# Feed-forward of a two-layer encoder: eight parts projected down one by one, or together by seven block products

## The chip, the cores and the metric

The kernel runs on one core of a Trainium2 chip. The metric is the device time of one execution in microseconds (us), the median of several runs. Engines are named as in the profile: PE is TensorE's matmul stream and PEld its weight loads, DVE is VectorE, ACT is ScalarE, POOL is GpSimd, SP is SyncE, which here issues all the DMAs on one queue in order. Every engine works through its own instructions in a fixed order and waits where an operand or a buffer is not there yet.

## The reference, cut to what matters

A two-layer encoder, width 1024, is applied to a prompt of 256 tokens and a sample of 512. Each layer modulates its normalised input by a condition (adaptive norm), runs a mixer (layer 0: mLSTM; layer 1: windowed attention), adds it, normalises and modulates again, and runs a feed-forward with a convolution over the tokens:

```
def conv_ffn(h, w_up, conv_w, conv_b, w_down):
    u = h @ w_up
    u = lax.conv_general_dilated(u, conv_w[:, None, :], window_strides=(1,),
                                 padding=((CONV_WIDTH // 2, CONV_WIDTH // 2),),
                                 ...
    g = u[..., :D_FF]
    val = u[..., D_FF:]
    return (jax.nn.silu(g) * val) @ w_down
```

`D_FF` is 2816, the convolution is three tokens wide and works per channel, all values are float32. The result is added to the stream with a gate from the condition.

## The kernel before, in words

**Layout.** Activations lie with channels on the 128 partitions and the 768 tokens of both sequences along the free axis. A float32 product is made from three matmuls in a format of fewer bits: both operands are split into a high part (a cast on ACT, L260) and a low part (a subtraction on DVE, L261), and PE adds high x high, high x low and low x high (L254, or L1169, L1170, L1172 in the up projection).

**Weights** lie in DRAM in units of 128 x 2048, loaded as two halves of 128 x 1024 (512 KB, L269) into a ring of five buffers called `raw`, and split into rings of three `whi` and three `wlo`. Other rings: `slab` (six large buffers), `nt` (eight of 128 x 384 or so), and in PSUM four `pa` buffers in turn and four banks, in the feed-forward at fixed places.

**Feed-forward.** The 2816 channels of each of gate and value are cut into 11 parts (`NPART`) of 256 + 256. `up(p)` makes a part's projection, convolution, gate and product; `down(p)` multiplies the product's 256 channels by the part's unit of down weights and adds the 1024 x 768 result to the stream. The loop at the end of `ffn` runs `down` one part behind `up`: up(0), up(1), down(0), up(2), down(1), ..., up(10), down(9), down(10).

`up` of parts 1 to 10 is made of two `pair`s. A pair takes a 2 x 2 block view of the product (two rows of 128 channels, the inner dimension in two halves of 512, the tokens in two halves of 384) and makes it by seven block products in place of eight (Strassen's scheme in Winograd's form). The seven weight operands come from POOL (four additions and subtractions of 128 x 512, L1202, L1205, L1206, L1214), the seven token operands were made once in the layer's head. A pair is seven `quarters` of 12 matmuls of 384 columns; ACT copies PSUM banks on between them (L1218, L1223, L1229, L1240) and evicts rows (L1182), DVE adds two rows (L1242, L1243). `conv` is one activation on ACT (L1387) and two multiply-adds on DVE (L1389, L1390) per row; `silu` (L1397) is issued inside the next pair; `product` multiplies gate and value on POOL (L1402, 128 x 772) and splits the result on ACT and DVE (L260, L261).

`down(p)` below part 10 loads and splits two weight tiles and runs, for 8 blocks of output channels, 512 sample and 256 prompt tokens, 2 x 3 matmuls; each of the 16 results in PSUM is added to the stream by one DVE instruction (`resid`, L590). `down(10)` goes over three ranges of 256 tokens and starts the next norm.

**What sets the order.** Inside the head of the feed-forward and inside the attention's blocks the PE order is written by hand; elsewhere a list scheduler places each engine's instructions from the program's order and its own estimates, once, when the kernel is built. SP's queue is in order too: a DMA that waits for a buffer or for data holds all later ones.

**The mixers.** The mLSTM has a loop over four heads; in it, while the projections of q and k run, steps of the adaptive norm's weights for later (`adaln_g`, `adaln_v`: loads of 512 KB and multiply-adds on DVE, L506) are issued by `self.step(...)`. POOL does small operations there: masks (L708), powers of the normalisation (L826), products with the output gate (L850). The attention goes over 48 steps of blocks, in which scores, transposes and values of a block are three steps apart (`LAG`), and POOL normalises each block's probabilities (L1000).

## Time and profile before

| | |
|---|---|
| median of 3 runs | 1844.86 us (1842.9 to 1848.7) |
| the profiled execution | 1843.78 us |
| its span, first to last instruction | 1842.0 us |
| busy in the span: PE, DVE, ACT, POOL | 97%, 74%, 49%, 26% |
| mean granted clock of PE | 0.994 |
| DMA | 184.48 MB, mean 100 GB/s |

The stages lie in the span like this (stretches that were cut by eye, with the busy time of the engines in each):

| stretch, us | what | PE | DVE | ACT | POOL |
|---|---|---|---|---|---|
| 0 to 38 | start | 22.7 | 12.5 | 11.9 | 8.9 |
| 38 to 505 | mLSTM and adaptive norms | 459.2 | 328.6 | 205.5 | 47.1 |
| 505 to 548 | output projection, head of feed-forward 0 | 41.9 | 37.3 | 22.2 | 9.3 |
| 548 to 1043 | feed-forward 0 | 489.9 | 390.4 | 241.2 | 180.5 |
| 1043 to 1230 | attention | 184.1 | 130.7 | 122.3 | 53.5 |
| 1230 to 1340 | output projection, head of feed-forward 1 | 107.4 | 81.1 | 56.0 | 12.8 |
| 1340 to 1842 | feed-forward 1 | 488.0 | 386.4 | 236.2 | 176.0 |

How to read the lines of the profile. A window's row gives its length and, for each engine, the busy time and the number of instructions, then the granted clock of PE (1.00 is full), the share of the DMA engines' time and GB/s. A group's row gives the line of the kernel, engine, operation, output <- inputs, the shape, the count, the busy time in us, the mean of one in ns, and behind the last bar the engine's idle time ahead of these instructions with what ended it. A timeline's row gives start, duration, engine, line and operation, and in brackets the idle time ahead of it. A DMA row gives the number, the size and the median us from issue to landing. Matmuls overlap in PE's pipeline, so that the distance of two starts, and not a duration, is what one costs.

### The profile page before, as it was taken

The page shows a single profiled execution, that of the slowest core. Times are in us where ns is not written, and L with a number is a line of the kernel's source. Part 1 is how long each engine was busy: PE and PEld are TensorE (multiplying, and loading weights), DVE is VectorE, ACT ScalarE, POOL GpSimd, SP SyncE. Part 2 cuts the span into 40 slices and gives each one's busy share as a digit, 9 for nine tenths or more (in the row PEclk, how much of TensorE's full clock was granted, in tenths as well). Part 3 has the DMA queues.
Part 4 walks back from the last instruction along what each step waited for, and adds up shares of the span by engine and source line. Part 5 has one row for each costly group of instructions (what it writes and reads, how often), then busy time and mean ns, then how long its engine had stood idle before and what let it go on. Part 6 is the DMA issues. An engine that isn't in the chain of part 4 may idle for free.

```text
span 1842.0 us, 28931 instructions
## 1 busy us (share of the span) xinstructions
PE 1793.2 (97%) x11290; PEld 1657.4 (90%) x11290; DVE 1367.0 (74%) x2101; ACT 895.3 (49%) x1815; POOL 488.0 (26%) x386
## 2 busy tenths in 40 slices
PE   6999999999999999999999999999999999999997
PEld 3987887889998999999999999889989999999997
DVE  4755676886689877777777757766898777777776
ACT  4443443354456444444444556765564444444443
POOL 1001001021024333333331313430144333333322
PEclk9999999999999999999999999999999999999999
DMA  8344566546312221222223321124122222222212
GB/s 330 119 145 134 172 195 221 164 138 219 101 46 74 76 61 66 69 69 69 69 69 93 104 83 50 53 94 129 50 86 69 69 69 69 69 69 70 69 35 69
DMA packets 64245, 184.48 MB, mean 100 GB/s; under 512 B 6167, under 2 KB 23831, under 8 KB 64108
## 3 DMA queue, kind: packets, MB, share of 16 engines
q1 hardware_dynamic: 64108, 182.63, 30.8%
q8 instruction: 89, 1.46, 0.3%
q14 instruction: 48, 0.39, 0.1%
HBM read 176.17 MB, written 6.43 MB: 99 GB/s over the span
## 4 chain that ended last, share of the span: by engine, by line
PE 86%; DVE 6%; DMA 3%; ACT 2%; issue 1%; POOL 1%; SPq 0%; POOLq 0%; ACTq 0%; DVEq 0%
PE ps L254 27%; PE pa L254 25%; PE ps L1169 10%; PE ps L1172 10%; PE ps L1170 10%; PE pa L1008 1%; DMA slab<-in_adaln_w_dram 1%; DMA raw<-in_w_dram 1%; DVE wlo L261 1%; DVE ada L506 1%; DVE slab L590 1%; DMA raw<-in_adaln_w_dram 0%; PE pa L1172 0%; PE pa L1169 0%; PE pa L1170 0%
## 5 line engine op out<-in xcount | busy, mean ns | idle before, releaser
L260 ACT CAST whi<-raw 128x1024 fp32r<-128x1024 f32 x237 | 247.9, 1048 | 350.4 <-PE pa L254 161.4
L261 DVE TENSOR_TENSOR wlo<-raw,whi 128x1024 fp32r<-128x1024 f32 x237 | 316.6, 1337 | 119.8 <-ACT whi L260 117.3
L254 PE MATMUL pa<-slab,whi 128*128 128x256 f32 (+1 forms) x1472 | 346.6, 331 | 3.2 <-DVE slab L590 3.2
L254 PEld LDWEIGHTS pa<-slab,whi 128*128 128x128 f32 x1472 | 252.7, 188 | 27.5 <-DVE slab L590 4.5
L590 DVE SCALAR_TENSOR_TENSOR slab<-pa,mod,slab 128x256 f32<-128x256 f32 (+1 forms) x368 | 211.2, 592 | 70.8 <-PE pa L254 70.5
L254 PE MATMUL pa<-slab,wlo 128*128 128x256 f32 (+1 forms) x736 | 233.9, 330 | 0.0
L254 PE MATMUL ps<-zh,whi 128*128 128x256 f32 (+1 forms) x560 | 189.0, 339 | 2.3 <-ACT whi L260 1.7
L254 PE MATMUL ps<-zh,wlo 128*128 128x256 f32 (+1 forms) x560 | 184.1, 330 | 2.0 <-DVE wlo L261 2.0
L254 PE MATMUL ps<-zl,whi 128*128 128x256 f32 (+1 forms) x560 | 185.1, 332 | 0.0
L1169 PE MATMUL ps<-zh,whi 128*128 128x384 f32 x504 | 172.3, 342 | 3.6 <-ACT nt L1240 1.8
L1170 PE MATMUL ps<-zl,whi 128*128 128x384 f32 x504 | 169.9, 337 | 0.8 <-DVE zl L1126 0.8
L1172 PE MATMUL ps<-zh,wlo 128*128 128x384 f32 x504 | 168.9, 335 | 0.0
L254 PEld LDWEIGHTS pa<-slab,wlo 128*128 128x128 f32 x736 | 138.5, 188 | 13.1 <-DVE wlo L261 0.4
L1205 POOL TENSOR_TENSOR raw<-raw,raw 128x512 f32<-128x512 f32 x40 | 52.2, 1305 | 330.8 <-DVE wlo L261 259.4
L254 PE MATMUL ps<-slab,whi 128*128 128x384 f32 x512 | 132.0, 339 | 0.9 <-DVE slab L261 0.5
L1402 POOL TENSOR_TENSOR slab<-slab 128x772 f32<-128x772 f32 x44 | 86.5, 1967 | 164.6 <-DVE slab L1390 152.7
L1389 DVE SCALAR_TENSOR_TENSOR slab<-slab,cstt,slab 128x771 f32<-128x771 f32 x88 | 103.6, 1179 | 26.6 <-ACT slab L1387 26.5
L254 PEld LDWEIGHTS ps<-zh,whi 128*128 128x128 f32 x560 | 107.4, 192 | 15.9 <-issue 4.4
L506 DVE SCALAR_TENSOR_TENSOR ada<-raw,silc,ada 128x1024 f32<-128x1024 f32 x84 | 110.6, 1354 | 14.9 <-DMA raw<-in_adaln_w_dram 14.8
L1202 POOL TENSOR_TENSOR raw<-raw 128x512 f32<-128x512 f32 x40 | 68.5, 1712 | 200.1 <-DMA raw<-in_w_dram 169.7
L254 PEld LDWEIGHTS ps<-zh,wlo 128*128 128x128 f32 x560 | 107.2, 192 | 12.2 <-DVE wlo L261 2.9
L254 PEld LDWEIGHTS ps<-zl,whi 128*128 128x128 f32 x560 | 107.4, 192 | 11.9 <-issue 3.4
(291 smaller groups left out, 4265.7 us busy)
## 6 DMA issues: line engine op xcount, KB each, us to landing
raw<-in_w_dram SPq DMA_DIRECT2D x208, 512.0 KB, 3.7
raw<-in_adaln_w_dram SPq DMA_DIRECT2D x84, 512.0 KB, 4.6
slab<-in_x_dram SPq DMA_DIRECT2D x12, 512.0 KB, 6.8
slab<-in_adaln_w_dram SPq DMA_DIRECT2D x12, 512.0 KB, 10.3
slab<-mrows SPq DMA_DIRECT2D x8, 384.0 KB, 5.3
xs<-slab SPq DMA_DIRECT2D x6, 512.0 KB, 3.6
bt<-brow SPq DMA_DIRECT2D x16, 192.0 KB, 3.0
slab<-xs SPq DMA_DIRECT2D x6, 512.0 KB, 6.9
```

The costliest lines, as they stand in the source:

```text
L254: self.nc.tensor.matmul(out, lhsT, rhs, start=start, stop=stop)
L260: nc.scalar.copy(hi, src)
L261: return nc.vector.tensor_tensor(lo, src, hi.bitcast(F32), ALU.subtract)
L506: stt(acc[:, s], row, w, acc[:, s], ALU.mult, ALU.add)
L590: self.nc.vector.scalar_tensor_tensor(x, o, self.mod[l][:, gc + c, q : q + 1], x, ALU.mult, ALU.add)
L1169: mm(o, wh[:, k], hi[k], start=start and k == 0, stop=False, skip_group_check=True)
L1170: mm(o, wh[:, k], lo[k], start=False, stop=False, skip_group_check=True)
L1172: mm(o, wl[:, k], hi[k], start=False, stop=k == 3, skip_group_check=True)
L1202: tt(q[2], q[2], q[3], ALU.add)
L1205: tt(q[0], q[2], q[0], ALU.subtract)
L1389: stt(y[:, 1:], u[:, :-1], w(0), y[:, 1:], ALU.mult, ALU.add)
L1402: nc.gpsimd.tensor_tensor(y, y, yrow[:, j], ALU.mult)
```

## The change

Parts 0, 1 and 10 keep their `down`. For parts 2 to 9 (`SOLO` = 2, `NBLK` = 8) it is replaced:

- `sums(l)` makes, on POOL, the four weight operands of Winograd's form for each of the eight units of down weights, in the `raw` ring, and stores them to a DRAM scratch `sd`. It is spread over the mixer: layer 0's in the mLSTM's loop (five steps with each q or k of heads 1 and up), layer 1's in the attention (one step per block from the third).
- `operands(yrow, k)` takes the place of `product` in these parts: POOL multiplies gate and value (four instructions), DVE makes four sums, and the seven token operands of the part (128 x 7 x 384) are stored to a DRAM scratch `yd`.
- `blocked` runs after the last pair: seven block products, each over the eight parts, for four blocks of output channels and 384 tokens, 96 matmuls each. It loads weights (from the weights as they are, or from `sd`) and operands from `yd`, splits them on ACT and DVE, keeps sums in eight PSUM buffers, and adds the results to the stream.
- Then comes `down(10)`. The PE order inside `blocked` is written by hand.

The diff, without the lines of constants that stand in the text above:

```diff
                     if h:
                         self.step(self.fillp)
+                        self.step(self.fills, 5)
                 qk.append(t)
...
         done = 0
+        extra = self.sums(1)
         with self.tc.manual_schedule(engines={mybir.EngineType.PE}):
...
                 if x < nb:
                     scores(blocks[x])
+                if x > 1:
+                    next(extra, None)
                 if LAG <= x < nb + LAG:
                     flip(blocks[x - LAG])
...
+        for _ in extra:
+            pass
         return act
...
+    def sums(self, l):
+
+        nc = self.nc
+        tt = nc.gpsimd.tensor_tensor
+        self.sd[l] = sd = self.dp.tile([NBLK, P, 2048], F32, name=f"sd{l}")
+        for k in range(NBLK):
+            u = U_FFN + (l * NPART + SOLO + k) * 3 + 2
+            r = [self.load(u, h) for h in range(2)]
+            s2, s4, s1, s3 = (t[:, 512 * i : 512 * (i + 1)] for t in r for i in range(2))
+            yield
+            tt(s1, s1, s3, ALU.add)
+            yield
+            tt(s2, s1, s2, ALU.subtract)
+            yield
+            tt(s4, s4, s2, ALU.subtract)
+            nc.sync.dma_start(sd[k, :, :1024], r[0])
+            yield
+            tt(s3, s3, s2, ALU.subtract)
+            nc.sync.dma_start(sd[k, :, 1024:], r[1])
+            yield
+
+    def blocked(self, l, xt, u, yd):
+
+        nc = self.nc
+        w, sd = self.io["w"], self.sd[l]
+
+        def given(i):
+            return lambda k: w[u + 3 * k : u + 3 * k + 4 : 3, :, 512 * i : 512 * (i + 1)]
+
+        def summed(i):
+            return lambda k: sd[k : k + 2, :, 512 * i : 512 * (i + 1)]
+
+        stream = [
+            (given(0), 0), (given(1), 2), (summed(0), 4), (summed(1), 3), (summed(3), 1), (summed(2), 6), (given(3), 5),
+        ]
+        K = range(NBLK)
+        parts = {}
+
+        def ready(i):
+            if i >= len(stream):
+                return
+            src, z = stream[i]
+            ys = self.slab([P, NBLK, H])
+            for k in K[::4]:
+                nc.sync.dma_start(ys[:, k : k + 4], yd[k : k + 4, :, z].rearrange("k p t -> p k t"))
+            for k in K:
+                if k % 2 == 0:
+                    raw = self.stg.tile([P, 2, 512], F32, tag="raw", name=self.nm("raw"), bufs=5)
+                    nc.sync.dma_start(raw, src(k).rearrange("k p c -> p k c"))
+                    wt = self.split(raw.rearrange("p k c -> p (k c)"))
+                y = [self.tmp([P, H], R) for _ in range(2)]
+                self.fp_copy_split(*y, ys[:, k])
+                parts[i, k] = [t[:, 512 * (k % 2) : 512 * (k % 2 + 1)] for t in wt], y
+
+        X = [self.pa()[:, :H] for _ in range(4)]
+        Y = [self.bank[c][:, :H] for c in range(4)]
+
+        def add(c, c0, o):
+            for p0, p1, q in pieces(c0, c0 + H):
+                self.resid(xt, o[:, p0 - c0 : p1 - c0], l, 40, c, (p0, p1, q))
+
+        late = [(c, k) for k in K[:-2] for c in range(4)] + [(c, k) for c in range(4) for k in K[-2:]]
+        soon = [(c, k) for c in range(4) for k in K[:2]] + [(c, k) for k in K[2:] for c in range(4)]
+        steps = [
+            (X, late, True, lambda c: nc.scalar.copy(Y[c], X[c])),
+            (X, soon, False, lambda c: add(c, 0, X[c])),
+            (Y, late, False, lambda c: nc.scalar.copy(X[c], Y[c])),
+            (Y, soon, False, lambda c: add(c, H, Y[c])),
+            (X, late, False, lambda c: add(c + 4, H, X[c])),
+            (Y, late, True, lambda c: (add(c, H, Y[c]), add(c + 4, H, Y[c]))),
+            (X, late, False, lambda c: add(c + 4, 0, X[c])),
+        ]
+        mm = nc.tensor.matmul
+        for i, (o, order, start, done) in enumerate(steps):
+            for j in (0, 1) if i == 0 else (i + 1,):
+                ready(j)
+            with self.tc.manual_schedule(engines={mybir.EngineType.PE}):
+                for c, k in order:
+                    (wh, wl), (yh, yl) = parts[i, k]
+                    cs = slice(c * P, (c + 1) * P)
+                    mm(o[c], wh[:, cs], yh, start=start and k == 0, stop=False, skip_group_check=True)
+                    mm(o[c], wh[:, cs], yl, start=False, stop=False, skip_group_check=True)
+                    mm(o[c], wl[:, cs], yh, start=False, stop=k == K[-1], skip_group_check=True)
+                    if k == K[-1]:
+                        done(c)
...
+        yd = self.dp.tile([NBLK, P, 7, H], F32, name=f"yd{l}")
+
+        def operands(yrow, k):
+
+            s = self.slab([P, 7, H])
+            for j in range(2):
+                row = s[:, 2 * j : 2 * j + 2].rearrange("p z t -> p (z t)")
+                for p0, p1, _ in pieces(0, T):
+                    b = slice(col(p0), col(p0) + p1 - p0)
+                    nc.gpsimd.tensor_tensor(row[:, p0:p1], yrow[:, 2 + j, b], yrow[:, j, b], ALU.mult)
+            b11, t3, b21, b22, t2, t4, t1 = (s[:, z] for z in range(7))
+            tt = nc.vector.tensor_tensor
+            tt(t3, b22, t3, ALU.subtract)
+            tt(t2, b11, t3, ALU.add)
+            tt(t4, b21, t2, ALU.subtract)
+            tt(t1, b22, t2, ALU.subtract)
+            nc.sync.dma_start(yd[k], s)
+
...
-            g = self.slab([P, 2, 2, TG], R)
+            g = None if SOLO <= p < SOLO + NBLK else self.slab([P, 2, 2, TG], R)
...
-            if p:
+            if g is None:
+                operands(yrow, p - SOLO)
+            elif p:
                 product(yrow, g)
...
             if prev is not None:
                 down(*prev)
-            prev = (p, g)
+            prev = (p, g) if g is not None else None
+        self.blocked(l, xt, u0 + 3 * SOLO + 2, yd)
         down(*prev)
...
+        self.fills = self.sums(0)
         act = self.mlstm(pool, gates, xt)
-        for _ in chain(self.fillp, self.fill):
+        for _ in chain(self.fillp, self.fill, self.fills):
             pass
```

More of the change, by code (lines that the diff above doesn't have):

```diff
@@ L35 @@
 NPART = FC // 2
+SOLO = 2
+NBLK = 8
 EPS = 1e-6
@@ L184, in __init__ @@
         self.early, self.begun = {}, {}
+        self.sd = {}
     def start(self, rng, gen):
```

## Prediction

> **What bounds the kernel now.** I read the page's first part, then the windows of the feed-forward's steady stretch, then the single instructions.
>
> ```profile
> span 1842.0 us, 28931 instructions
> ...
> PE 1793.2 (97%) x11290; PEld 1657.4 (90%) x11290; DVE 1367.0 (74%) x2101; ACT 895.3 (49%) x1815; POOL 488.0 (26%) x386
> ```
>
> PE is busy 97% of the span, so time is won only where PE has less to do, and lost wherever PE is made to wait. The windows show three consecutive parts of feed-forward 0, and, for later, the two mixers.
>
> ```profile
> core 0: us, PE busy (x) PEld busy (x) DVE busy (x) ACT busy (x) POOL busy (x), PEclk, DMA share, GB/s
> 623.50:669.90 46.40, 46.20 (x264) 43.88 (x263) 34.34 (x40) 21.30 (x35) 16.40 (x10) 1.00 0.20 65
> 669.90:716.34 46.44, 46.44 (x265) 44.03 (x265) 35.08 (x40) 21.50 (x35) 16.50 (x10) 1.00 0.22 69
> 716.34:762.75 46.41, 46.41 (x265) 43.99 (x265) 35.76 (x42) 21.56 (x35) 17.42 (x10) 1.00 0.23 68
> 124.00:300.00 176.00, 171.74 (x1210) 146.46 (x1210) 116.72 (x214) 71.78 (x196) 11.68 (x9) 0.99 0.54 172
> 300.00:412.00 112.00, 110.21 (x740) 96.69 (x739) 92.23 (x139) 49.43 (x120) 18.61 (x14) 1.00 0.54 177
> 1096.00:1215.00 119.00, 118.41 (x989) 106.99 (x988) 90.15 (x285) 85.93 (x285) 46.27 (x80) 1.00 0.18 52
> ```
>
> A part takes 46.4 us and PE has no gap in it. The same holds, within a few per cent, in the mLSTM (124 to 412) and in the windowed attention (1096 to 1215): whatever the change puts there must stay off PE's path.
>
> **The matmuls.** The change removes `down` for eight parts of each layer and adds seven block products, each of 8 parts x 4 output blocks x 3 = 96 matmuls of 384 columns. The trace has such matmuls in the up projection; from the first row below to the last lie 66 steps, (661.92 − 650.36)/66 = 0.175 us each.
>
> ```profile
> 650.36 0.34 PE L1169 MATMUL ps<-zh,whi 128*128 128x384 f32 x1
> ...
> 661.92 0.34 PE L1170 MATMUL ps<-zl,whi 128*128 128x384 f32 x1
> ```
>
> A part's two pairs are 168 such matmuls: 29.4 us. The `down` beside them is what is left of the period, 46.4 − 29.4 = 17.0 us. Eight of them are 136.0 us; seven products are 7 x 96 x 0.175 = 117.6 us. So 18.4 us per layer are to be had, **36.8 us** for both: an eighth of the down work, less what is lost around it.
>
> **The stretch without down.** While parts 3 to 10 go up, nothing lies between two pairs any more, and everything else has 29.4 us in place of 46.4. One part's groups (669.90 to 716.34):
>
> ```profile
> L261 DVE TENSOR_TENSOR wlo<-raw,whi 128x1024 fp32r<-128x1024 f32 x8 | 11.3, 1415 | 5.5 <-ACT whi L260 5.3
> ...
> L260 ACT CAST whi<-raw 128x1024 fp32r<-128x1024 f32 x9 | 9.4, 1049 | 16.3 <-PE pa L254 8.4 <-PE ps L1170 4.1 <-POOL raw L1206 3.7
> ...
> L590 DVE SCALAR_TENSOR_TENSOR slab<-pa,mod,slab 128x512 f32<-128x512 f32 x8 | 5.9, 744 | 1.8 <-PE pa L254 1.8
> ...
> L1206 POOL TENSOR_TENSOR raw<-raw 128x512 f32<-128x512 f32 x2 | 3.9, 1954 | 0.1
> ...
> L1402 POOL TENSOR_TENSOR slab<-slab 128x772 f32<-128x772 f32 x2 | 3.7, 1856 | 6.4 <-DVE slab L1390 6.4
> ...
> L590 DVE SCALAR_TENSOR_TENSOR slab<-pa,mod,slab 128x256 f32<-128x256 f32 x8 | 3.7, 479 | 2.2 <-PE pa L254 2.2
> ...
> L1205 POOL TENSOR_TENSOR raw<-raw,raw 128x512 f32<-128x512 f32 x2 | 2.6, 1296 | 15.3 <-DVE wlo L261 15.3
> ...
> L261 DVE TENSOR_TENSOR slab<-slab,slab 128x772 fp32r<-128x772 f32 x2 | 2.3, 1174 | 0.0
> ...
> L260 ACT CAST slab<-slab 128x772 fp32r<-128x772 f32 x2 | 1.7, 830 | 0.5 <-POOL slab L1402 0.5
> ...
> L1242 DVE TENSOR_TENSOR slab<-ps,nt 128x384 f32<-128x384 f32 x2 | 1.1, 550 | 0.4 <-PE ps L1172 0.4
> ...
> L1223 ACT COPY nt<-ps 128x384 f32<-128x384 f32 x2 | 0.9, 475 | 0.0
> ```
>
> DVE loses 16 residual adds (9.6 us), two weight splits (2.8) and two operand splits (2.3), and gains four 128x384 subtractions or additions of 0.55: 35.1 − 14.7 + 2.2 = 22.6 of 29.4 us. ACT loses two weight casts and two operand casts: 21.5 − 3.8 = 17.7. POOL swaps two products (3.7) for four, two of 512 and two of 256 columns. The 512s cost 1.30 to 1.95 each by the two POOL rows, the 256s about half; that is 4 to 6, so 17 to 19 of 29.4. No engine becomes the bound. But PE waits for single tiles: the weight split that needs POOL's last sum had the whole `down` as cover and now has, worked out by hand in DVE's new order, some 2 us, and the PSUM copy in the middle of a pair stands on ACT behind a weight cast with almost none. I bound the stall by 0 (both in time) and 1.5 us a part (cast 1.05 plus copy 0.47, both bare), and take **0.2**, near the lower end, since PE shows no gap in the rows above with the same order within a pair: 16 x 0.2 = 3.2 us.
>
> **From the last pair into the block products.** Here PE has nothing of its own to fill with: before, `down(9)` lay there; now product 0 follows the pair directly, in PE's written order. By the new instruction order, product 0's first token cast on ACT stands behind the two operand casts of part 10, these wait for POOL's two products, and the second of those for the convolution of the last row. The load of product 0's token operands is on SP's queue behind two weight loads, the second of which waits for the split of the pair's last weight tile. The same chain stands in the trace of before at the end of layer 0's part 10, where `down(9)` hid it:
>
> ```profile
> 998.32 0.33 PE L1172 MATMUL ps<-zh,wlo 128*128 128x384 f32 x1
> ...
> 999.47 0.54 ACT L1182 COPY slab<-ps 128x128 f32<-128x128 f32 x2
> 1000.04 1.03 ACT L1387 ACTIVATE slab<-slab,cstt 128x772 f32<-128x772 f32 x1
> ...
> 1002.54 1.01 DVE L1389 SCALAR_TENSOR_TENSOR slab<-slab,cstt,slab 128x771 f32<-128x771 f32 x1
> ...
> 1006.06 1.00 DVE L1390 SCALAR_TENSOR_TENSOR slab<-slab,cstt,slab 128x771 f32<-128x771 f32 x1
> ...
> 1007.21 1.86 POOL L1402 TENSOR_TENSOR slab<-slab 128x772 f32<-128x772 f32 x1 [6.33 <-DVE slab L1390]
> ...
> 1009.10 0.84 ACT L260 CAST slab<-slab 128x772 fp32r<-128x772 f32 x1 [1.37 <-POOL slab L1402]
> ```
>
> From the pair's end (998.65) to 1009.94 that is 11.3 us. About 4 of them were DVE's residual adds in between, which are gone. Without them: 1001.07 convolution on ACT, +2.0 on DVE, +1.9 POOL, +0.85 cast, +0.48 token cast, +0.55 its low half on DVE: 6.9 + 1.4 = about 8.3 us from the pair's end to the first matmul. The load, from 2.4 us behind the pair's end (cast 1.05, split 1.25 to 1.4), lands by these rows:
>
> ```profile
> raw<-in_w_dram SPq DMA_DIRECT2D x208, 512.0 KB, 3.7
> ...
> slab<-mrows SPq DMA_DIRECT2D x8, 384.0 KB, 5.3
> xs<-slab SPq DMA_DIRECT2D x6, 512.0 KB, 3.6
> ```
>
> It is 768 KB behind 512 KB, in short runs: between 3.7 and twice 5.3 us, so 6 to 13 us behind the pair's end. Both ends meet around 9 us: **9 us per layer**, bounds 7 and 13. Then the clock:
>
> ```profile
> 40.00:42.00 2.00, 2.00 (x11) 2.00 (x11) 2.00 (x8) 2.00 (x5) 0.00 (x0) 0.50 0.63 252
> ...
> 1058.00:1061.00 3.00, 0.83 (x4) 0.84 (x5) 2.92 (x7) 2.96 (x9) 0.00 (x0) 0.89 0.00 0
> 1061.00:1064.00 3.00, 3.00 (x17) 3.00 (x16) 2.90 (x7) 1.40 (x4) 0.00 (x0) 0.54 0.32 85
> ```
>
> After a gap of 2.2 us the next 3 us ran at 0.54: (1 − 0.54) x 3 = 1.4 us lost. I take **1.5 us** per layer, bounds 0 and 3. In sum 10.5 per layer, **21 us**. The Trainium skill ("TensorE: Matmul & The Clock Gate", section "Why this matters for your kernels") warns of PE gaps over about 3 us, after which the clock is at half until PE has been busy for a window of about 3.4 us; by that page the loss would be some 1.7 us a gap, an estimate, and the sum 0.4 us longer. The row at 1058 shows the drop after a shorter gap than that.
>
> **The products themselves.** Per 16.8 us a product wants 2 MB of weights and 1.5 MB of operands, 3.67 MB with KB of 1024, or 218 GB/s. That is more than the 172 to 177 of the mLSTM windows and less than the 252 of the window at 40. DVE has four weight splits, eight token splits and some adds (5.7 + 4.4 + 2 to 4), ACT 4.2 + 3.8 + 2, of 16.8 us. I take no stall; bounds 0 and, if only 177 GB/s came, 20.7 − 16.8 = 3.9 us for each of 14 products.
>
> **The sums of weights**, eight rounds per layer, each two loads of 512 KB into two of the five raw buffers, four POOL operations, two stores on SP. In the mLSTM:
>
> ```profile
> L826 POOL TENSOR_TENSOR ss<-ss,mhalf 128x4 f32<-128x4 f32 x4 | 4.1, 1014 | 164.2 <-DVE ss L825 115.1 <-DMA slab<-mrows 49.0
> ...
> L261 DVE TENSOR_TENSOR wlo<-raw,whi 128x1024 fp32r<-128x1024 f32 x24 | 29.3, 1220 | 9.3 <-ACT whi L260 9.2
> ```
>
> A round takes 3.7 + 4 x 1.3 to 1.95 + 3.6 = 12.5 to 15 us, while a weight tile is split every 288/24 = 12 us. SP's order puts two of the mixer's weight loads (heads 1 and 2, one each at the worst place) behind stores that wait for POOL's last sum; worked out by hand one of them comes about 3 us late in each head, the others in time. The small POOL powers (L826), on the path of a head's normalisation, queue behind sums of up to 1.95 us. Bounds 0 and 8 x 3 = 24 us; I take **5**. In the attention the 80 normalisations on POOL (46.3 of 119 us) share it with 32 sums (about 53): 99 of 119, and sums that wait for a load hold back the normalisations behind them. The blocks run three ahead, about 9 us (119/40 a block); bounds 0 and 10, I take **2.5**.
>
> **Sum**, from the profiled execution's 1843.78 us (1842.0 of span and 1.8 around it; the median of the runs is 1844.86, 0.06% more): −36.8 + 3.2 + 21 + 5 + 2.5 = −5.1, so **1838.7 us**. What a measurement of this kernel can tell from no change is about 0.3%, 5.5 us: faster is below 1839.3, slower above 1850.4. The forecast lies at the edge of the first.
>
> **Rivals.**
> *The transition at its floor*, the sums free. The chain without any queue is 7.3 us (0.54 + 1.03 + 2.0 + 1.86 + 0.84 + 0.48 + 0.55) and the clock might stay up: −36.8 + 3.2 + 14.6 = −19: 1825 us; with no stall up the parts, 1822. For it: POOL is busy 12 and 19 us of 176 and 112 in the mLSTM. Against it: the chain had 11.3 us, and the clock row.
>
> *Slower: weight loads of the mLSTM behind the stores of the sums.* If not two but all eight rounds delay a weight tile by 3 us, the mLSTM loses 24 in place of 5: 1857.7 us. It turns the sign from 16.7 us on, 2.1 us a round. For it: five raw buffers, two held for 12.5 to 15 us, one in-order queue. Against: DMA share 0.54, and PE already waits there for little (4.3 of 176 us, 1.8 of 112).
>
> *Slower: the up stretch bound by single tiles.* POOL's busy share rises from 36% to about 61%. The 128x1024 split takes 1220 ns in the mLSTM, where POOL is busy 7 to 17%, and 1415 where it is 36%; at the same slope (195 ns for some 25 points) it would be about 1600, six a part, 1.2 us more per part on DVE, inside the 2 us. With 1.5 us of stall a part, 16 x 1.3 = 21 us more: 1859.5. The Trainium skill ("GPSIMD Engine Reference", section "1. Specifications") has GpSimd share its SBUF interfaces with VectorE, in contention with VectorE's instructions of two SBUF inputs, as this split is; the two rows agree with it.
>
> *The products bound by DMA*: 14 x 3.9 = 55 more, 1893.
>
> *The change doesn't do less work*: eight parts' 96 matmuls of 512 and 256 columns stand against 7 x 96 of 384 in the new order, so it does; I give it nothing.
>
> **Chances.** Forecast with its own bounds (1831 to 1849): 0.42, of which 0.20 below 1839.3 and 0.22 within. Transition at its floor (1815 to 1831): 0.20. mLSTM and attention queues (1850.4 to 1870): 0.22. Up stretch: 0.10. DMA: 0.06. So faster 0.40, same 0.22, slower 0.38. The range leaves out the DMA case and the far ends of the others: 1816 to 1868.
>
> **What would show it.** In the profile of the changed kernel: windows of a part from 3 to 10 at 29.4 to 29.9 us; two PE gaps of 7 to 13 us, ended by DVE's low half of a token operand or its load, followed by 3 us at a granted clock near 0.5; products of 16.8 us with PE unbroken; windows of the mLSTM about 5 us longer in sum, its new PE waits on weight splits; the attention 2 to 3 us longer. A PE gap between the pairs on `whi`/`wlo`, in the products on `raw`, or many in the mLSTM would prove the forecast wrong.

## The result, and the profile after

The change makes the kernel slower: 1922.6 us median of 4 runs (1919.7 to 1923.6) against 1844.8, a ratio of 1.0416, 95% interval 1.0396 to 1.0437. The forecast was 1838.7, with a range of 1816 to 1868, so the time lies 55 us past its end. Runs of one kernel lie within 0.3% (6 us) of each other; the versions further below ran once, except where a ratio with its interval is given.

In the changed kernel the old lines stand a little lower: L1227 is the PSUM copy in the middle of a pair (L1218 before), L1178 to L1181 the matmuls of the up projection, L257 most others, L1251 and L1252 the row additions, L1483 to L1486 the convolution, L263 and L264 the split, L272 the weight loads, L1498 the product of gate and value, L1510 the products of `operands` and L1513 to L1516 its sums, L1211 to L1223 POOL's weight operands of a pair, L1266 to L1274 the sums of weights (stores at L1271 and L1274), L1337 to L1339 the block products. In the attention L1002 and L1004 normalise a block and L1012 transposes it. A row of waits says who waited for whom: us in total, how often, the longest.

The head of the profile after:

```profile
span 1917.9 us, 29330 instructions
...
PE 1789.0 (93%) x11098; PEld 1677.8 (87%) x11098; DVE 1372.9 (72%) x2077; ACT 953.8 (50%) x1935; POOL 594.2 (31%) x482
```

PE is idle for 129 us in place of 49, and its busy time hardly falls, since part of it is now at half clock (granted clock 0.972 in the mean, 0.994 before). Cut at the first matmuls of the stretches, the 75.9 us of span go here:

| stretch | before | after | more |
|---|---|---|---|
| start to the first up projection (mLSTM in it) | 510.1 | 538.6 | +28.5 |
| feed-forward 0, to the end of the products (before: of down(9)) | 505.6 | 524.4 | +18.8 |
| from there to the attention's transposes | 82.5 | 88.0 | +5.5 |
| attention, and to the next up projection | 202.4 | 208.0 | +5.6 |
| feed-forward 1, as above | 506.2 | 523.0 | +16.8 |
| rest | 35.2 | 35.9 | +0.7 |

Three stretches of the up projection without `down`, and two of the products, as windows:

```profile
800.00:834.00 34.00, 30.76 (x167) 30.36 (x166) 25.33 (x24) 17.81 (x31) 18.89 (x13) 0.95 0.30 103
834.00:868.00 34.00, 31.18 (x170) 30.85 (x169) 26.28 (x24) 17.62 (x31) 16.27 (x13) 0.95 0.31 103
868.00:902.00 34.00, 31.01 (x169) 30.68 (x168) 26.24 (x24) 17.48 (x31) 16.69 (x12) 0.95 0.31 103
...
960.50:977.20 16.70, 16.70 (x99) 16.70 (x98) 9.06 (x13) 9.32 (x16) 0.00 (x0) 1.00 0.66 223
977.20:994.00 16.80, 16.80 (x98) 16.80 (x98) 11.62 (x21) 8.31 (x13) 0.00 (x0) 1.00 0.65 222
```

A part takes about 34 us where 29.4 to 29.9 were forecast: some 3 us of idle PE and 0.05 x 34 = 1.7 us of lost clock. A product takes 16.7 to 16.8 us with PE unbroken, as forecast, at 222 GB/s.

**The gap in each part.** In the timeline, from POOL's multiplications to the matmul that waited:

```profile
809.80 1.89 POOL L1211 TENSOR_TENSOR raw<-raw 128x512 f32<-128x512 f32 x1 [2.13 <-DMA raw<-in_w_dram]
811.66 1.97 POOL L1510 TENSOR_TENSOR slab<-slab 128x512 f32<-128x512 f32 x2
813.59 1.61 POOL L1214 TENSOR_TENSOR raw<-raw,raw 128x512 f32<-128x512 f32 x1
...
812.98 1.07 DVE L1513 TENSOR_TENSOR slab<-slab 128x384 f32<-128x384 f32 x1 [2.43 <-POOL slab L1510]
813.97 0.54 DVE L1252 TENSOR_TENSOR slab<-ps,nt 128x384 f32<-128x384 f32 x1
814.44 1.18 DVE L1514 TENSOR_TENSOR slab<-slab 128x384 f32<-128x384 f32 x1
815.73 1.46 DVE L1515 TENSOR_TENSOR slab<-slab 128x384 f32<-128x384 f32 x1
817.11 1.65 DVE L1516 TENSOR_TENSOR slab<-slab 128x384 f32<-128x384 f32 x1
818.68 0.54 DVE L1251 TENSOR_TENSOR slab<-ps,nt 128x384 f32<-128x384 f32 x1
...
819.31 1.03 ACT L1483 ACTIVATE slab<-slab,cstt 128x772 f32<-128x772 f32 x1 [1.46 <-DVE slab L1251]
820.25 1.03 ACT L263 CAST whi<-raw 128x1024 fp32r<-128x1024 f32 x1
...
821.60 0.48 ACT L1227 COPY ps<-ps 128x384 f32<-128x384 f32 x1
...
822.14 0.69 PE L1178 MATMUL ps<-zh,whi 128*128 128x384 f32 x1 [3.24 <-ACT ps L1227]
```

PE names the copy L1227, but the copy waited for nothing of its own. Read upwards: the copy stands on ACT behind a weight cast, that behind a convolution, which waits for the row addition L1251 on DVE, which stands behind the four sums of token operands. These take 0.55 us each where POOL is idle, and here 1.07 to 1.65. The first of them had waited 2.43 us for POOL's multiplications, and these stand on POOL behind a weight operand that had waited 2.13 us for its load.

**The transition** of layer 0:

```profile
936.49 2.47 POOL L1498 TENSOR_TENSOR slab<-slab 128x772 f32<-128x772 f32 x1 [17.20 <-ACT slab L1483]
939.92 2.57 POOL L1498 TENSOR_TENSOR slab<-slab 128x772 f32<-128x772 f32 x1 [0.96 <-ACT slab L263]
...
937.33 2.45 DVE L1486 SCALAR_TENSOR_TENSOR slab<-slab,cstt,slab 128x771 f32<-128x771 f32 x1
...
942.53 0.83 ACT L263 CAST slab<-slab 128x772 fp32r<-128x772 f32 x1 [2.70 <-POOL slab L1498]
943.27 1.75 ACT L263 CAST nt<-slab 128x384 fp32r<-128x384 f32 x4
```

The forecast chain in the forecast order. PE waits 10.6 us (933.3 to 943.8); DVE's and POOL's steps take 2.45 and 2.57 in place of 1.0 and 1.86, side by side. Then the clock, in a window behind the gap:

```profile
943.80:949.00 5.20, 4.81 (x16) 4.41 (x17) 2.44 (x6) 1.73 (x4) 0.00 (x0) 0.57 1.06 401
```

0.43 x 5.2 = 2.2 us: 13 us per layer in all.

**The mLSTM.** PE's waits from 38 to 540 us, and one of them in the timeline:

```profile
PE ps L257 <- ACT whi L263: 9.5, 2, 5.0
PE ps L257 <- DVE wlo L264: 8.5, 4, 4.3
PE pa L837 <- ACT hs L833: 3.9, 1, 3.9
```

```profile
234.61 1.23 SPq L1274 DMA_DIRECT2D sd<-raw  x1
239.34 2.85 SPq L272 DMA_DIRECT2D raw<-in_w_dram  x3
...
247.03 1.04 ACT L263 CAST whi<-raw 128x1024 fp32r<-128x1024 f32 x1 [4.72 <-DMA raw<-in_w_dram]
...
248.12 0.80 PE L257 MATMUL ps<-zh,whi 128*128 128x512 f32 x1 [5.05 <-ACT whi L263]
```

The first two sorts were 1.7 and 2.0 us before. SP gets past the store of a sum at 235.8 and issues no load until 239.3; the weight tile lands at 247 and PE has waited 5 us. What SP waited for is its own row of waits, from 234 to 241 us: a load into a `raw` buffer that a sum's store had not yet left.

```profile
SPq L272 <- DMA sd<-raw: 3.5, 1, 3.5
```

There are six gaps over 2.5 us between 120 and 275 us, and with each of them the clock falls; from 240 to 260 us it is 0.74 in the mean.

**The attention's** waits have one long one, for a normalisation on POOL, which also makes the weight sums there:

```profile
PE pa L1012 <- POOL t L1004: 5.0, 1, 5.0
```

```profile
1143.81 0.17 DVE L1002 RECIPROCAL st<-st 128x2 f32<-128x2 f32 x1 [0.51 <-ACT t L998]
...
1147.85 1.26 POOL L1266 TENSOR_TENSOR raw<-raw 128x512 f32<-128x512 f32 x1 [7.82 <-DMA raw<-in_w_dram]
...
1150.43 0.94 POOL L1004 TENSOR_SCALAR t<-t,st 128x256 f32<-128x256 f32 x2
```

The normalisation could have run at 1144.0, behind DVE's reciprocal. It stands on POOL behind two weight sums, the first of which waits 7.8 us for its load.

### The profile page after: what moved, and what is told of

The parts are those of the page before. It is cut to its first block, busy times and chain, and to the rows that moved or that the text cites. A ratio compares the mean times of both kernels' runs of the same rounds, so it can differ in the third digit from the quotient of the medians.

```text
span 1917.9 us, 29330 instructions
## 1 busy us (share of the span) xinstructions
PE 1789.0 (93%) x11098; PEld 1677.8 (87%) x11098; DVE 1372.9 (72%) x2077; ACT 953.8 (50%) x1935; POOL 594.2 (31%) x482
## 4 chain that ended last, share of the span: by engine, by line
PE 62%; DVE 13%; DMA 11%; ACT 5%; POOL 4%; issue 4%; SPq 0%; POOLq 0%; ACTq 0%; DVEq 0%
PE ps L257 20%; PE pa L257 9%; PE ps L1178 6%; PE ps L1179 6%; PE ps L1181 6%; DMA raw<-in_w_dram 5%; DMA raw<-in_adaln_w_dram 3%; DVE wlo L264 3%; PE pa L1338 2%; PE pa L1339 2%; PE pa L1337 2%; PE ps L1339 2%; PE ps L1337 2%; PE ps L1338 2%; DVE ada L509 2%
## 5 line engine op out<-in xcount | busy, mean ns | idle before, releaser
L264 DVE TENSOR_TENSOR wlo<-raw,whi 128x1024 fp32r<-128x1024 f32 x261 | 350.9, 1347 | 125.5 <-ACT whi L263 125.0
L263 ACT CAST whi<-raw 128x1024 fp32r<-128x1024 f32 x261 | 272.5, 1047 | 236.1 <-PE ps L1179 54.7
L1178 PE MATMUL ps<-zh,whi 128*128 128x384 f32 x504 | 175.4, 348 | 34.7 <-ACT ps L1227 32.3
L257 PE MATMUL ps<-zh,whi 128*128 128x256 f32 (+1 forms) x560 | 192.3, 344 | 9.7 <-ACT whi L263 9.5
L257 PE MATMUL ps<-zh,wlo 128*128 128x256 f32 (+1 forms) x560 | 187.7, 337 | 8.1 <-DVE wlo L264 8.1
L257 PE MATMUL ps<-zl,whi 128*128 128x256 f32 (+1 forms) x560 | 188.2, 338 | 0.1
L1181 PE MATMUL ps<-zh,wlo 128*128 128x384 f32 x504 | 172.9, 343 | 0.0
L1178 PEld LDWEIGHTS ps<-zh,whi 128*128 128x128 f32 x504 | 97.5, 193 | 42.8 <-ACT ps L1227 38.8
L257 PE MATMUL ps<-slab,whi 128*128 128x384 f32 x512 | 132.2, 340 | 0.9 <-DVE slab L264 0.5
L257 PEld LDWEIGHTS ps<-zh,whi 128*128 128x128 f32 x560 | 109.9, 197 | 23.7 <-ACT whi L263 10.4
L1483 ACT ACTIVATE slab<-slab,cstt 128x772 f32<-128x772 f32 x88 | 91.0, 1035 | 78.1 <-DVE slab L1251 76.3
L1211 POOL TENSOR_TENSOR raw<-raw 128x512 f32<-128x512 f32 x40 | 61.2, 1531 | 217.1 <-DMA raw<-in_w_dram 206.4
L1485 DVE SCALAR_TENSOR_TENSOR slab<-slab,cstt,slab 128x771 f32<-128x771 f32 x88 | 106.4, 1210 | 30.1 <-ACT slab L1483 29.9
L257 PEld LDWEIGHTS ps<-zh,wlo 128*128 128x128 f32 x560 | 109.3, 195 | 18.9 <-DVE wlo L264 9.2
L257 PEld LDWEIGHTS ps<-zl,whi 128*128 128x128 f32 x560 | 109.7, 197 | 14.1 <-issue 4.6
L1510 POOL TENSOR_TENSOR slab<-slab 128x512 f32<-128x512 f32 x64 | 92.8, 1471 | 58.8 <-DVE slab L1486 41.4
L263 ACT CAST nt<-slab 128x384 fp32r<-128x384 f32 x112 | 56.8, 512 | 108.4 <-PE pa L1338 61.5
L264 DVE TENSOR_TENSOR nt<-slab,nt 128x384 fp32r<-128x384 f32 x112 | 60.7, 554 | 67.3 <-ACT nt L263 67.3
L1337 PE MATMUL pa<-nt,whi 128*128 128x384 f32 x256 | 87.9, 343 | 21.1 <-ACT nt L263 21.1
L1181 PE MATMUL ps<-yh,wlo 128*128 128x384 f32 x304 | 104.7, 344 | 1.9 <-DVE wlo L264 1.9
```

The source lines that it names most:

```text
L257: self.nc.tensor.matmul(out, lhsT, rhs, start=start, stop=stop)
L263: nc.scalar.copy(hi, src)
L264: return nc.vector.tensor_tensor(lo, src, hi.bitcast(F32), ALU.subtract)
L1178: mm(o, wh[:, k], hi[k], start=start and k == 0, stop=False, skip_group_check=True)
L1181: mm(o, wl[:, k], hi[k], start=False, stop=k == 3, skip_group_check=True)
L1337: mm(o[c], wh[:, cs], yh, start=start and k == 0, stop=False, skip_group_check=True)
```

## The experiments

Times are to be held against 1922.6 (changed) and 1843 to 1845 (before). "Start" is the first matmul of the first up projection: 510.1 before, 538.6 changed. A gap is idle time of PE.

**Without the sums of weights.**

```diff
-        self.fills = self.sums(0)
+        self.fills = iter(())
...
-        extra = self.sums(1)
+        extra = iter(())
```

> Leaves out the sums of down weights: no loads, POOL operations and stores for them in the mixers; the block products read the plain weights in their place (so the output isn't the reference's). Theory: the mLSTM's 28 us and the attention's 6 us are the price of the sums, and nothing else in them: the start of the first feed-forward comes back from 538.6 to 510 us, the attention from 141.7 to 136.4 us, the whole to about 1888 us. Rival: part of the loss in the mLSTM is a new order of the other instructions that the scheduler chose; then some of the 28 us stays.

Measured 1886.2, 36 us less. Start 510.7 and attention 136.4, both as before the change: the sums are the whole price in the mixers, and nothing else of the change adds to it there. The two stretches as windows:

```profile
38.00:510.00 472.00, 464.00 (x3132) 414.17 (x3133) 331.56 (x557) 206.71 (x481) 51.19 (x37) 0.99 0.49 159
1121.90:1258.30 136.40, 135.76 (x1156) 122.76 (x1158) 99.54 (x322) 95.81 (x323) 53.01 (x94) 1.00 0.20 59
```

**What of the sums costs: POOL, the queue, the buffers, the bytes.** Four edits of `sums`, their lines one behind the other: without its four `tt`; with POOL issuing the stores; without `tt` and with 32 of 1024 columns moved; and as copies from DRAM to DRAM, once free and once issued behind a weight split.

```diff
-            tt(s1, s1, s3, ALU.add)
...
-            nc.sync.dma_start(sd[k, :, :1024], r[0])
+            nc.gpsimd.dma_start(sd[k, :, :1024], r[0])
...
+            nc.sync.dma_start(sd[k, :, :32], r[0][:, :32])
...
+            nc.sync.dma_start(sd[k, :, :1024], self.io["w"][u][:, :1024])
```

> The sums of down weights without their POOL operations: the same loads into the raw ring and the same stores, of plain weights (so the output isn't the reference's). Theory (the ring and SP's queue are the price in the mLSTM: weight loads wait behind stores and for buffers): at least two thirds of the mLSTM's 28 us stay, the first feed-forward starts at 530 to 540 us, the whole 1910 to 1922 us. Rival (POOL's 54 us of additions are: they hold up the small powers on POOL and slow VectorE beside them): most of it goes, 510 to 518 us, the whole 1888 to 1900 us.

> The stores of the weight sums are issued by POOL, behind the addition that they wait for, in place of SP. Theory (loads held on SP behind stores that wait for POOL): the mLSTM loses 5 to 15 us of its 28, since the ring is still shared and a store's landing still sets a buffer free; the whole 1905 to 1917 us. Rival (the ring alone): no change within 3 us. Rival (POOL's time): slower, since POOL also issues the stores.

> The rounds of the weight sums take their two raw buffers and their places on SP's queue as before, but each load and store moves 32 of 1024 columns, and POOL does nothing (the block products read plain weights, so the output isn't the reference's). Theory (buffers: two of five raw buffers are out of the ring for a load and a store's time, and SP's queue waits for them): two thirds of the mLSTM's 28 us stay or, since a small load and store are faster, at least 12 us; first feed-forward from 522 us or later. Rival (bytes: 2 MB a round beside loads at 172 GB/s): it goes, 510 to 515 us.

Measured 1927.3, 1922.0 and 1909.5; start at 537.3, 537.4 and 526.5. Without POOL's additions the start moves by 1.3 us, and with the stores off SP by 1.2: so POOL's time is not the price of 28.5 us, nor is the stores' wait for POOL on SP's queue. Differences as small as these can't be read off the starts: versions below that leave `sums` to the mixers as it is and change the feed-forwards alone start anywhere from 534.3 to 544.9, since the scheduler orders the whole program anew. 16 us stay although nothing is computed and almost nothing is moved: they are the price of two of five raw buffers together with the places in the queue, which no edit takes apart. The other 11 come with the full transfers, which also hold the buffers longer.

The attention became slower in the first and the third edit (151.2 and 144.6 us against 141.7), although POOL makes no sums there. In the first, PE waits 8.0 us in one place, behind a DVE operation that waits for the attention's own load of a bias (`bt`), which SP had issued behind a round's loads and stores:

```profile
1167.45 0.48 DVE L993 CUSTOM_DVE_ANT_0 t<-pa,bt,nsk 128x256 f32<-128x256 f32 x1 [10.30 <-DMA bt<-brow]
```

So the transfers and their places in the queue can cost as much there as the sums on POOL; how the attention's price divides between them stays open.

> The rounds of the weight sums as copies from DRAM to DRAM: the same bytes read and written at the same places of the program, without raw buffers, without POOL and without waits on either (plain weights, so the output isn't the reference's). Theory (buffers): the mLSTM comes back to 515 us or less at the start of the first feed-forward, the attention to 137 us. Rival (bytes): it stays at 530 us or more.

> The weight sums' bytes as copies from DRAM to DRAM once more, each now issued behind a weight split of the mixer, so that they are spread over it and do not all start in the first 90 us (plain weights, no raw buffers, no POOL; the output isn't the reference's). Theory (buffers 16, bytes 12 of the mLSTM's 28 us): first feed-forward from 520 to 526 us. Rival (buffers alone): 510 to 514 us; rival (bytes alone): 535 us or more. Attention: 137 us if buffers are its price.

Measured 1920.5 and 1919.7, start 546.0 and 546.1. Neither answers the question: in both, all 32 copies of both layers were issued between 30 and 87 us, since nothing that they wait for held them, and PE waited 27 and 29 us for one weight tile behind them (the row is of the first):

```profile
86.67 0.58 PE L257 MATMUL ps<-zh,whi 128*128 128x256 f32 x1 [27.26 <-ACT whi L263]
```

The issue order asked for in the second did not hold them back. Whether the 11 us are bytes or the time that a buffer is held stays open.

**The gap in each part.** Left out first DVE's four sums, then POOL's four multiplications as well; and, apart from these, `operands` issued half a pair later.

```diff
-            tt(t3, b22, t3, ALU.subtract)
-            tt(t2, b11, t3, ALU.add)
-            tt(t4, b21, t2, ALU.subtract)
-            tt(t1, b22, t2, ALU.subtract)
...
-                operands(yrow, p - SOLO)
+                held.append(lambda: operands(yrow, p - SOLO))
```

> Leaves out the four sums of token operands per part on DVE (the block products read the four plain products in their place, so the output isn't the reference's); POOL's four multiplications stay. Theory: the gap of about 3 us once a part, on the PSUM copy L1227, comes from these four DVE operations, which stand ahead of the row addition L1251, which the convolution on ACT awaits, behind which the copy stands: without them no gap over 1 us in the parts 3 to 10, idle 20.6 to 5 us and half clock 6.8 to 0 per layer, 2 x 21 = 42 us less, about 1880 us. Rival: POOL's multiplications ahead of the weight sums delay the weight tile itself: then the gaps stay and the time moves by less than 10 us.

> Leaves out POOL's four multiplications and DVE's four sums of a part; the value rows are stored and read in the operands' place (so the output isn't the reference's). Theory: without DVE's sums a gap of 1.17 us a part was left, on the same copy, behind a weight cast that waits for POOL's sums, which stand behind POOL's multiplications: it goes too, idle time of the up stretch 12.5 to 5 us per layer, some 15 us less than without DVE's sums alone, 1868 to 1872 us. Rival: the 1.17 us is the weight load's own lateness (POOL waits 2.3 us for raw there): then 1880 us or more.

> Issues a part's operands (POOL's products and DVE's sums) behind the PSUM copy in the middle of the next pair, where silu already stands, in place of the pair's end. Theory (DVE's sums ahead of the row addition and the convolution are the price): the gaps go, 35 to 42 us less, 1880 to 1888 us, with two more slabs' worth of waiting at the end of part 9. Rival (POOL's queue): the products now stand ahead of the second pair's weight sums and the gaps move there; no change or slower.

Measured 1885.2, 1871.7 and 1931.3. PE's waits in feed-forward 0's up projection, changed kernel, without DVE's sums, without both:

```profile
PE ps L1178 <- ACT ps L1227: 16.7, 8, 3.3
```

```profile
PE ps L1178 <- ACT ps L1227: 8.6, 7, 2.0
```

```profile
PE ps L1178 <- ACT ps L1227: 2.2, 3, 1.1
```

Both theories hold a share. DVE's sums make the gaps 2.1 to 3.3 us in place of 1.2, and half clock comes with the longer ones only (with 8 of the 10 in both layers; without the sums the up projection has none): 15 to 17 us per layer. POOL's multiplications ahead of the weight operands are the last 1.2 us a part, 7 to 9 us per layer. The third edit did not move the gap: DVE's sums stand at the same place in its order, since in the changed kernel they already came that late; it tells only that a place in the program is not a place on the engine. Its 9 us more than the changed kernel lie elsewhere, 5 of them ahead of the start.

**The transition.**

```diff
-SOLO = 2
+SOLO = 1
```

> The blocked parts are 1 to 8 in place of 2 to 9, so that down(9) lies between the last pair and the first block product; the same matmuls in sum. Theory: each transition of the changed kernel costs a PE gap of 10.6 us (933.3 to 943.8 and 1752.1 to 1762.6) and about 5 us at half clock, because the first token cast stands on ACT behind the chain of the pair's last row; 17 us of down(9) cover all of it: 2 x 15 = 30 us less, about 1892 us. Rival: the gap is the landing of the token operands, whose load now also stands behind down(9)'s two weight loads: then a gap of 5 us or more stays ahead of the first product and the time is 1905 us or more.

Measured 1924.9. The theory of the transition holds: PE idles 0.9 us in all from the last pair to the first product, the clock stays up and seven products take 117.3 us in place of 119.2. The time does not fall, against the expectation, which had forgotten that one more part now goes up without `down`: seven gaps of 2.2 to 3.3 us per layer in place of five, with half clock behind 10 of the 14, and the mLSTM, in another order, starts the feed-forward 6 us later.

**Other places for the sums.** The operand sums go into the products: a part stores its four plain products, and POOL makes the other operands in place, in 20 operations of 128x768 per layer, while PE runs the products. Then the multiplications go to DVE.

```diff
+        def less(r, k, z):
+            ...
+            nc.sync.dma_start(raw[:, :, :H], yd[k : k + 2, :, z].rearrange("k p t -> p k t"))
+            pt(ys[r][:, k : k + 2], ys[r][:, k : k + 2], raw[:, :, :H], ALU.subtract)
...
-                    nc.gpsimd.tensor_tensor(row[:, p0:p1], yrow[:, 2 + j, b], yrow[:, j, b], ALU.mult)
+                    nc.vector.tensor_tensor(row[:, p0:p1], yrow[:, 2 + j, b], yrow[:, j, b], ALU.mult)
```

> A version that computes the reference: parts 1 to 8 blocked, so that down(9) covers the start of the products; only the four plain products of a part are stored; the other three operands are made by POOL, in place, during the block products, in 20 operations of 128x768 per layer, where POOL is idle. Theory: the transition costs 2 us in place of 16, and the up stretch has the 1.2 us gap a part alone: 1922 less 2 x 14 and 2 x 15, with one more gap each: 1864 to 1870 us; all that is left over 1845 is the mixers' 34 us and those gaps. Rival: POOL beside DVE in the products slows the token casts, so that the products are no longer 16.8 us each: 1880 us or more.

> As the version with operand sums inside the products, but a part's four multiplications are on DVE in place of POOL (computes the reference). Theory: they take 2.3 us of DVE's slack per part and no longer delay POOL's weight sums, so the 1.18 us gap per part goes: 7 x 2 x 1.2 = 16 us less, 1860 to 1864 us. Rival: on DVE they stand ahead of the row addition, as the operand sums did, and leave a gap of about their own length, 1 to 2 us: 1874 us or more.

Measured 1878.2 and 1861.7. The first missed by 8 us: with POOL beside the products seven of them take 122 us in place of 117.3, and PE waits there for the low halves of token operands on DVE, 5.1 us in all (the last section shows what POOL does to these). With the multiplications on DVE the gap of 1.2 us a part is gone and two pairs take 29.5 us. The mixers' price, 31 us to the start and 12 around the attention, is now more than both layers gain; so the next versions put block products into layer 1 alone, with its weight sums in the attention (`layer1`), and behind parts 1 to 8 of feed-forward 0 (`layer1f`); both layers once more, each with its sums in its own up projection (`own`); and layer 1 alone with its sums behind parts 2 to 9 of feed-forward 0 (`layer1g`, whose edit is shown).

```diff
             g = up(p)
+            if l == 0 and SOLO < p <= SOLO + NBLK:
+                self.step(self.later, 5)
```

> That version with the block products in layer 1 alone; layer 0 projects down part by part and the mLSTM holds no sums (computes the reference). Theory: the mLSTM's 28 us go, and layer 0 is as before the change; what is left is the attention's 6 us against the feed-forward's 18.4 less 5 for the products beside POOL and 1 to 3 for the up stretch: 1834 to 1840 us, faster than before the change. Rival: with the multiplications on DVE the up stretch still loses a us a part: 1843 us or more.

> As the version with block products in layer 1 alone, but its eight rounds of weight sums stand in layer 0's feed-forward, one behind each of the parts 1 to 8, where POOL is a third busy and DMA a fifth, in place of the attention (computes the reference). Theory: the attention comes back to 136.4 us and the way to it to 99.6, 10 to 14 us less; the up projection of layer 0 loses 0 to 4 us: 1833 to 1838 us, below the kernel before the change. Rival (the raw ring is no freer there, two pairs and a down use all five buffers): the loss moves into layer 0's parts, 1843 us or more.

> Both layers with block products (parts 1 to 8, operand sums inside the products, multiplications on DVE); each layer's eight rounds of weight sums stand in its own up projection, one behind each of the parts 1 to 8; the mixers hold none (computes the reference). Theory: the mixers are as before the change, each feed-forward gains 18.4 less 5 for the products; the parts, at 29.5 us with PE unbroken, have room for a round (POOL 6.6 us more, two of five raw buffers for some 13 us): lost 0 to 1 us a part, 1818 to 1834 us. Rival (the raw ring: two pairs take four of its buffers in 29.5 us, and a round's two come on top): a gap of 2 to 3 us and a half clock window a part, 16 x 4 = 64 us more, 1880 us or more.

> As the version with layer 1's block products and its weight sums in layer 0's feed-forward, but the rounds stand behind the parts 2 to 9 in place of 1 to 8, out of the stretch where part 1 has no cover (there a gap of 3.0 us and a half clock window were left; computes the reference). Theory: both go, 4 to 5 us less, 1833 to 1835 us. Rival: the gap is from the schedule around part 1 and stays: 1837 to 1839 us.

Measured, in this order, 1846.3 (one run), 1838.5 (ratio 0.9964, 0.9950 to 0.9977), 1895.0 (1.0271, 1.0256 to 1.0285) and 1830.7 (0.9927, 0.9914 to 0.9939), the last 2 us below its expectation and faster than both kernels. In the first the attention and the way to it lost 14 us, more than the 6 expected, and the up projection nothing. Moved into layer 0's feed-forward, where `down` lies between the pairs, the same eight rounds cost 4.7 us, and 0 behind the right parts. In an up projection without `down` they cost 32 and 40 us per layer; the waits of that kernel:

```profile
PE ps L1178 <- ACT ps L1227: 27.0, 16, 3.3
PE ps L1181 <- DVE wlo L264: 15.3, 12, 2.1
```

Whether raw buffers or POOL are short there these runs don't separate. The last version, the head of its profile and two parts of layer 1:

```profile
span 1828.8 us, 29103 instructions
...
PE 1776.6 (97%) x11194; PEld 1657.3 (91%) x11194; DVE 1389.3 (76%) x2089; ACT 926.8 (51%) x1875; POOL 532.8 (29%) x422
```

```profile
1406.00:1435.50 29.50, 29.50 (x171) 29.50 (x170) 23.30 (x25) 18.13 (x32) 11.22 (x8) 1.00 0.30 101
1435.50:1465.00 29.50, 29.50 (x170) 29.50 (x170) 23.24 (x25) 17.99 (x31) 10.62 (x8) 1.00 0.29 101
```

PE has no gap and DVE is busy 23.2 of 29.5 us, close to the 22.6 of the forecast. Feed-forward 1 takes 492.3 us to the end of the products, against 506.2: 13.9 us won, about 18.4 less 4.7 for the products beside POOL.

## Why the prediction was wrong, point by point

- **Matmuls: right.** 0.175 us each, 29.4 us a part, 16.8 us a product at 222 GB/s; the gain is there in `layer1g`, 13.9 of 18.4 us. DMA does not bound the products.
- **The stretch without `down`: the step that failed most**, 24 and 22 us in the two layers in place of 1.6. (The table's 18.8 and 16.8 us more, and the 18.4 that were to be won, less 13 for the transition.) It took 0.2 us a part since PE showed no gap in the rows before; but those rested on an order that the change alters. The wait it named, the copy on ACT, is the one that came, but its bound of 1.5 us counted ACT's own work and left out what stands ahead on DVE, four added sums in front of a row addition, and POOL's multiplications ahead of these. The sums' 2.2 us were booked as DVE's share of busy time, where they cost nothing, and not on the chain; and they were priced by a row addition with one input in PSUM (L1242, 0.55 us), while beside POOL they took 5.4 us a part. The rival of single tiles had the right place and about half of the size: 1.5 us a part, against 23/8 = 2.9.
- **The clock** was priced at the transition alone. The gaps of 2.1 to 3.3 us in the parts bring it too: 0.95 in the stretches shown, 7 to 8.5 us per layer, which the 24 and 22 contain.
- **The mLSTM: mis-sized**, 28.5 us in place of 5. That was the first slower rival, with its 24 us. Worked out by hand, one load came late in each of two heads; the trace has six gaps over 2.5 us, and the half clock with them, which the 5 us left out. Of the cause, 16 us are the rounds' two buffers and their places in the queue, taken together; the stores' wait for POOL, on which the working by hand rested, is not the bulk.
- **The attention: mis-sized**, 11 us in place of 2.5, a little past its bound of 10. The mechanism that it named, a sum that waits for its load and holds back the normalisation behind it, is the one in the longest gap, 5.0 us; but it stands ahead of the first transposes, where the blocks' lead of 9 us did not cover it; and the runs without POOL's sums show a second price, that of the transfers and the queue.
- **The transition: right in place and order**, 13 us per layer in place of 10.5, within its bounds of 7 to 16. (Its 6.9 + 1.4 us are 7.1 + 1.0 by its own rows, the same 8.)
- The errors are 43 us up the parts, 23.5 in the mLSTM, 8.5 in the attention, 5 in the transitions and 0.7 in the rest: 81 us, the whole miss of the profiled execution (1919.7 against 1838.7). The first three were taken near the end at which the cover holds, and each rival moved one term alone: the mLSTM and the parts at their rivals' prices together give 1838.7 + 19 + 20.8 = 1878.5, past the range already, and no chance was given to that.

## What to carry to other kernels

When an edit takes work from the bounding engine, the covers of everything beside it shrink with it: walk the new order of each engine from the added instruction to the next one that PE waits for, and price the chain, not the engine's share. Price a gap with the half clock that can follow it. Put a side job where the main work has the longest cover; eight rounds of the same size cost 28 us in the mLSTM, 14 in and before the attention, 32 to 40 in an up projection without `down`, and nothing in one with it. A wait names the last link, so read upwards until a link has waited for nothing.

## What the runs showed of the hardware

DVE operations with two inputs in SBUF took up to three times as long while POOL computed; those with an input in PSUM did not. L1516, a subtraction of 128x384 in SBUF, has a minimum, a median and a maximum (ns) of

```profile
L1516 DVE TENSOR_TENSOR slab<-slab x16: 545/1643/1651, 670.1 to 1735.3; 128x384 f32<-128x384 f32 x16
```

The two of 0.55 us are those of the first part of each layer, where POOL is idle; the 14 others run beside POOL. The row addition L1252, of the same size with one input in PSUM, took 0.54 us at 813.97, while POOL ran as well. The split of token operands, in the products of the changed kernel (POOL idle) and of the version with the multiplications on DVE (POOL makes operands beside them):

```profile
L264 DVE TENSOR_TENSOR nt<-slab,nt 128x384 fp32r<-128x384 f32 x112 | 60.7, 554 | 67.3 <-ACT nt L263 67.3
```

```profile
L264 DVE TENSOR_TENSOR nt<-slab,nt 128x384 fp32r<-128x384 f32 x112 | 101.2, 924 | 24.4 <-ACT nt L263 24.2
```

In the mLSTM, two operations that POOL's weight sums cover until 232.3 (4.37 us), and one alone:

```profile
229.02 4.37 DVE L509 SCALAR_TENSOR_TENSOR ada<-raw,silc,ada 128x1024 f32<-128x1024 f32 x2 [2.85 <-DMA raw<-in_adaln_w_dram]
...
234.63 1.27 DVE L509 SCALAR_TENSOR_TENSOR ada<-raw,silc,ada 128x1024 f32<-128x1024 f32 x1
```

Not every one is slowed: at 939.86 a split of 128x772 took 0.96 us beside a multiplication on POOL, which took 2.57 in place of 1.86. The forecast had taken 195 ns from means over stretches in which the two engines meet only part of the time. The Trainium skill ("GPSIMD Engine Reference", section "1. Specifications") names this contention for VectorE's instructions of two SBUF inputs, and these rows agree; the sizes are from the rows.

How long PE idles does not alone decide whether the clock falls. In the kernel before, half clock followed the gap of 2.2 us ahead of 1060 us (0.54 from 1061 to 1064). In `own` PE idled 3.25 us ahead of 656.1 and the granted clock stayed at 1.00 from 640 to 674 us.
